# Score products of two attention stages on 128 partitions instead of 64

## The chip, the cores and the metric

The kernel runs on one core of a Trainium2 chip. The metric is the device time of one execution, in microseconds (us), as the median of several runs. TensorE is the matrix engine (PE in the profile, PEld for its weight loads), VectorE is DVE, ScalarE is ACT, GpSimd is POOL, and SyncE (SP) issues most DMAs.

## What is computed

Three blocks on 256 latent tokens (and, in the first layer, 256 context tokens) of 1024 features, all in float32: two layers of a modulated network, then one layer with a hybrid mixer. Two parts matter here.

The first is the differential attention of layer 0. It has 8 heads, each with two maps of 64 features:

```
q, k, v = split(t @ w_in)                    # q, k: 8 heads x 2 maps x 64; v: 8 heads x 128
q, k    = rope(q), rope(k)                   # latent tokens only
sc      = einsum('blhid,bkhid->bihlk', q, k_all) * 64**-0.5
p       = softmax(sc);  p = p[:, 0] - lam * p[:, 1]
o       = rmsnorm(p @ v_all) * (1 - lambda_init)
```

The second is the mixer of the last layer, with 12 heads of 64 features in three groups of 4 (a causal window of 128, strides 4 and 16; four outputs that each join one head of every group) and 8 heads of block attention, which at 256 tokens is plain causal attention:

```
qa, ka, va, qb, kb, vb, g_a, g_b = split(h @ w_in)   # qa, ka, va: 12 x 64; qb, kb, vb: 8 x 64
scores = q @ k.T * 64**-0.5 - slope * distance, masked; softmax; @ v
merged = sigmoid(g_a) * (y_a @ w_up_a) + sigmoid(g_b) * (y_b @ w_up_b)
x      = x + merged @ w_out
```

## The kernel before

Every float32 operand of a product is kept as an exact sum hi + lo of two float32r parts. `split` and `split_scaled` (lines 115 to 122) make them: ACT copies the source to hi, DVE subtracts hi from the source for lo. `mm3` (lines 124 to 128) then forms a product as three matmuls that add up in one PSUM bank: hi hi, hi lo and lo hi. The profile puts these three at L126, L127 and L128, whoever calls them, so they are told apart by tile names and shapes. The shape `64*128 64x256` is a product that contracts over 64 partitions, has 128 weight columns and streams 256 columns.

SBUF tiles of 4 KB per partition come from one arena of 34 buffers (`unit`), PSUM tiles (`ps`) are 8 banks. The program is written in phases. A planner at compile time lays out each engine's queue, close to the order of the source; it puts an instruction that would have to wait behind the next one that need not.

**Differential attention** (`DiffAttention`, from line 861). A head's q and k come from TensorE with features on partitions: 128 partitions are the two maps of 64. `rope_in` and `rope_out` call `parts` once for the 256 context columns (from PSUM) and once for the 256 rotated latent columns (from SBUF), which lays out the operands of the scores. q of map 0 is `[hi0; lo0]` (hi on partitions 0 to 63, lo on 64 to 127), of map 1 `[lo1; hi1]`; k is `[lo0; hi0]`, `[hi1; lo1]`, and `r.hi = [hi0; hi1]`. So one product over 128 partitions (L1015) gives q_hi k_lo + q_lo k_hi, and a second over the 64 partitions of the map (L1016) gives q_hi k_hi:

```
nc.tensor.matmul(sc[:, 0:w], q[:, sb, tq], kk[:, sb, tk], start=True, stop=False)      # L1015
nc.tensor.matmul(sc[:, 0:w], q[pr, sb, tq], khi[pr, tk], start=False, stop=True)       # L1016
```

`scores` runs for 32 items: 8 heads, 2 streams (512 keys for latent queries, 256 for context), 2 tiles of 128 queries. Each item has two maps, and so four products. In every step of the pipeline come `scores` of an item, then `between` (a piece of the projections of later heads, or another filler), `turn` of the item before (transposed probabilities), `values`, and the norm of the output. POOL does a multiplication of the rotation (L943) and the power of the norm (L359).

**Hybrid mixer** (`HybridMixer`, from line 1300). `project` makes 128 columns of x @ w (two heads) with features on partitions, 24 matmuls of 256 columns. `qk` (in `body`) splits them into hi and lo tiles of 128 partitions, one ACT and one DVE instruction a block. 8 such blocks run ahead of the attention, 12 as the fillers of its steps 0 to 11 (`todo`, `each`). `scores` (L1360 to 1374) calls `mm3` on the 64 partitions of one head, `pr = slice(base, base + 64)`. There are 24 items: 16 with one head (the 8 block heads, two query tiles each, 128 or 256 keys), then 8 with three heads that share a softmax, and so nine products on 64 partitions one behind the other. POOL zeroes the ten tiles of v (L1419) at the start of `body`; `place` writes into the first four of them.

Of the kernel before, what the change touches and what calls it, by code (L numbers as in the profile page):

```python
# [13 lines left out]
P = 128  # L14
# [14 lines left out]
class Split:  # L29
    """A float32 operand as an exact sum hi + lo of two float32r parts.  # L30

    Both parts lie in 4 KB/partition units, `kpu` blocks of `width` columns each.
    """
# [25 lines left out]
class Order:  # L59
    """Pieces of independent chains, issued in the order of the times they are due at."""  # L60
# [16 lines left out]
class Kern:  # L77
# [41 lines left out]
    def split_scaled(self, hi, lo, src, scale):  # L119
        """scale: an immediate or a [P,1] column"""  # L120
        self.nc.scalar.activation(hi, src, AF.Copy, scale=scale)
        self.nc.vector.scalar_tensor_tensor(lo, src, scale, hi.bitcast(F32), ALU.mult, ALU.subtract)
# [13 lines left out]
    def wsplit(self, raw, arena=False):  # L136
        """(hi, lo) units"""
# [12 lines left out]
    def wdma256(self, w, c0):  # L150
        """256 columns of a [1024, n] matrix as two halves of the rows: 2 x [P, 4, 256]"""
# [5 lines left out]
    def wcols(self, w, c0, nk=KB):  # L157
        """128 columns of a [128 nk, n] matrix: [P, nk, 128]"""
        return self.wload(w[:, c0:c0 + P].rearrange("(k p) c -> p k c", p=P), [P, nk, P])

    def wrows(self, w, k, arena=False):
        """128 rows of a [n, 1024] matrix: [P, 1024]"""
        return self.wload(w[k * P:(k + 1) * P, :], [P, D], arena)

    def wpair(self, w, kp, c0, n=512, arena=False):
        """256 rows, up to 512 columns: [P, 2, n]"""
# [5 lines left out]
    def setup(self):  # L172
# [6 lines left out]
        # conditioning vectors, as columns: [P, 8, 32], column 0 latent, 1 context  # L179
# [15 lines left out]
        # adds up the two accumulations of each of 2 x 2 rows: [128, shift/scale, stream]  # L195
        self.sel = cp.tile([P, 2, 2], F32, name="sel")
        # sums over the partitions into row 0 or 1
# [15 lines left out]
    def cols(self, src, n, name, rows=None):  # L213
        """n rows of 128 -> [P, n] columns"""
# [11 lines left out]
    def ada_group(self, i, gi, vector=False):  # L226
        """modulation columns 2048*gi ... of layer i, for both streams, as columns; vector: the
        products with each partition's conditioning values on the vector engine"""
# [53 lines left out]
        # whatever this group completes  # L282
# [7 lines left out]
    def fill(self, n=1):  # L290
        """advance the pending adaLN products by n steps"""
# [6 lines left out]
    def mod_a(self, i, j):  # L298
        """(1 + scale) * g_pre of sublayer j (0 ffn, 1 mixer, 2 ffn)"""
# [7 lines left out]
    def mod_g(self, i, j):  # L307
        """weight * gate * g_post of sublayer j"""
# [8 lines left out]
    def gate_rows(self):  # L317
        """the gate vectors that are due to DRAM, from where they can be spread over the partitions"""
# [10 lines left out]
    def spread(self, row):  # L329
        """a vector of 1024 in DRAM on every partition"""  # L330
# [22 lines left out]
    def rstd_of(self, ss, n, width):  # L353
        """(ss / n + eps) ** -0.5 on [P, width]"""
# [7 lines left out]
    def gated(self, h, y, g, half):  # L362
        """h += rmsnorm(y) * g, y as two PSUM halves, the first complete `half` us before the second"""
# [30 lines left out]
    def begin(self, lT, nk, nt, w, tail):  # L394
        """y = lT.T @ w per token tile, whose last `tail` blocks wait for contract()"""
# [22 lines left out]
    def contract(self, c, residual, nxt):  # L418
        """the rest of c; residual(t, y) takes each tile, and nxt starts under the last blocks"""
# [1242 lines left out]
```

## Time and profile before

| | |
|---|---|
| time, median of 3 runs | 2371.59 us (2371.04 to 2375.98) |
| the profiled execution, its span | 2375.7 us |
| TensorE busy | 2331.7 us, 98% |
| VectorE, ScalarE, GpSimd busy | 1373.8, 996.8, 71.7 us |
| differential attention, `scores` | about 480 to 670 us |
| hybrid mixer, first block of `qk` to the last `scores` | about 1975 to 2118 us |

Start times are from the beginning of the span. A matmul's busy time runs from the first column to the modelled end of its last, and successive ones overlap; what a product costs a stage is the distance from its start to the start of the next.

### The profile page before, as it was taken

Reading aid. Unit: us, or ns where it says so; the run is one execution under the profiler, and the core shown is the slowest. Engines: PE = TensorE matmul, PEld = TensorE weight load, DVE = VectorE, ACT = ScalarE, POOL = GpSimd, SP = SyncE. Lnnn points to the kernel's source line nnn. Section 1 sums busy time; section 2 is a strip of 40 time slices with the busy share of each in tenths; the row PEclk is TensorE's granted clock in tenths of the full one; section 3 lists DMA queues with packets and bytes.
Section 4 is the critical chain, followed back from the end, with each engine's and each line's share of the span. In section 5 each row is a group of like instructions: output and inputs, shape, how many; then the busy total and the mean of one; then the engine's idle time right before and its main releaser. Section 6 shows DMA issues by size and latency. Waiting matters only on the chain.

```text
span 2375.7 us, 33808 instructions
## 1 busy us (share of the span) xinstructions
PE 2331.7 (98%) x13435; PEld 1993.5 (84%) x13435; DVE 1373.8 (58%) x2234; ACT 996.8 (42%) x1775; POOL 71.7 (3%) x104
## 2 busy tenths in 40 slices
PE   7999999999999999999999999999999999999998
PEld 5888788887678788888887887689989989998997
DVE  3866324577757663236766326675565556677554
ACT  4322223456544232224222225665445545555443
POOL 0000000001100000000000000100000001000000
PEclk9999999999999999999999999999999999999999
DMA  9655333312663652342655342445665675436654
GB/s 278 204 173 178 119 101 121 99 57 69 210 206 126 184 166 92 106 140 69 198 179 160 107 142 63 139 148 174 194 196 164 187 244 152 138 109 199 176 179 142
DMA packets 270951, 361.46 MB, mean 152 GB/s; under 512 B 11473, under 2 KB 222281, under 8 KB 270793
## 3 DMA queue, kind: packets, MB, share of 16 engines
q1 hardware_dynamic: 270464, 359.17, 48.8%
q8 instruction: 105, 1.72, 0.3%
q14 instruction: 54, 0.43, 0.1%
q10 hardware_dynamic: 328, 0.14, 0.0%
HBM read 355.02 MB, written 4.24 MB: 151 GB/s over the span
## 4 chain that ended last, share of the span: by engine, by line
PE 61%; DVE 4%; DMA 2%; ACT 1%; issue 1%; POOL 1%; POOLq 0%; DVEq 0%; ACTq 0%
PE ps L126 20%; PE ps L127 20%; PE ps L128 20%; DMA raw<-in_ffn_gate_dram 1%; DVE u L117 1%; DMA raw<-in_ada_w_dram 1%; ACT junk L344 1%; DVE u L382 1%; POOL sm L350 1%; DVE s_l L527 0%; PE ps L516 0%; DVE u L504 0%; DVE wl L117 0%; DVE u L245 0%; DVE scr L372 0%
## 5 line engine op out<-in xcount | busy, mean ns | idle before, releaser
L117 DVE TENSOR_TENSOR wl<-raw,wh 128x1024 fp32r<-128x1024 f32 x458 | 550.5, 1210 | 529.9 <-ACT wh L116 528.4
L126 PE MATMUL ps<-s_h,wh 128*128 128x256 f32 (+1 forms) x2560 | 840.0, 329 | 2.8 <-DVE s_h L805 1.9
L127 PE MATMUL ps<-s_l,wh 128*128 128x256 f32 (+1 forms) x2560 | 832.6, 325 | 0.6 <-DVE s_l L527 0.2
L128 PE MATMUL ps<-s_h,wl 128*128 128x256 f32 (+1 forms) x2560 | 831.6, 325 | 0.0
L116 ACT ACTIVATE wh<-raw 128x1024 fp32r<-128x1024 f32 x458 | 474.5, 1047 | 576.3 <-PE ps L127 501.8
L126 PEld LDWEIGHTS ps<-s_h,wh 128*128 128x128 f32 x2560 | 487.4, 191 | 52.9 <-issue 5.4
L127 PEld LDWEIGHTS ps<-s_l,wh 128*128 128x128 f32 x2560 | 487.6, 190 | 41.5 <-DVE s_l L527 2.3
L128 PEld LDWEIGHTS ps<-s_h,wl 128*128 128x128 f32 x2560 | 487.3, 190 | 39.8 <-issue 0.2
L126 PE MATMUL ps<-wh,s_h 128*128 128x512 f32 (+1 forms) x976 | 366.5, 376 | 0.5 <-DVE s_h L526 0.4
L127 PE MATMUL ps<-wl,s_h 128*128 128x512 f32 (+1 forms) x976 | 363.0, 372 | 0.0
L128 PE MATMUL ps<-wh,s_l 128*128 128x512 f32 (+1 forms) x976 | 363.0, 372 | 0.0
L245 DVE SCALAR_TENSOR_TENSOR u<-raw,sc,u 128x1024 f32<-128x1024 f32 x154 | 192.1, 1280 | 90.3 <-DMA raw<-in_ada_w_dram 89.8
L126 PEld LDWEIGHTS ps<-wh,s_h 128*128 128x128 f32 x976 | 183.8, 188 | 35.5 <-ACT u L1018 0.8
L116 ACT ACTIVATE s_h<-scr 128x256 fp32r<-128x256 f32 (+1 forms) x144 | 74.0, 514 | 328.1 <-DVE scr L684 306.2
L128 PEld LDWEIGHTS ps<-wh,s_l 128*128 128x128 f32 x976 | 183.8, 188 | 32.2
L127 PEld LDWEIGHTS ps<-wl,s_h 128*128 128x128 f32 x976 | 183.9, 188 | 31.1
L127 PE MATMUL ps<-u,s_h 128*128 128x512 f32 (+1 forms) x312 | 116.7, 374 | 1.3 <-DVE u L117 1.3
L126 PE MATMUL ps<-u,s_h 128*128 128x512 f32 (+1 forms) x312 | 117.2, 376 | 0.0
L128 PE MATMUL ps<-u,s_l 128*128 128x512 f32 (+1 forms) x312 | 116.5, 373 | 0.0
L684 DVE TENSOR_TENSOR scr<-scr,ps 128x512 f32<-128x512 f32 (+1 forms) x120 | 67.6, 563 | 65.1 <-PE ps L128 65.1
L682 ACT ACTIVATE scr<-ps 128x512 f32<-128x512 f32 (+1 forms) x120 | 58.6, 492 | 107.5 <-PE ps L128 100.8
L117 DVE TENSOR_TENSOR s_l<-scr,s_h 128x256 fp32r<-128x256 f32 (+1 forms) x144 | 78.3, 544 | 33.8 <-ACT s_h L116 33.4
(176 smaller groups left out, 1892.2 us busy)
## 6 DMA issues: line engine op xcount, KB each, us to landing
raw<-in_ffn_w_in_dram SPq DMA_DIRECT2D x176, 512.0 KB, 4.8
raw<-in_ada_w_dram SPq DMA_DIRECT2D x144, 512.0 KB, 4.4
raw<-in_ffn_w_out_dram SPq DMA_DIRECT2D x88, 512.0 KB, 3.5
raw<-in_ffn_gate_dram SPq DMA_DIRECT2D x44, 512.0 KB, 4.9
raw<-in_ffn_up_dram SPq DMA_DIRECT2D x44, 512.0 KB, 4.8
raw<-in_ffn_down_dram SPq DMA_DIRECT2D x44, 512.0 KB, 4.5
raw<-in_w_in_dram SPq DMA_DIRECT2D x44, 512.0 KB, 3.8
raw<-in_da_w_in_dram SPq DMA_DIRECT2D x24, 512.0 KB, 4.0
```

Source lines behind the costliest of these rows:

```text
L116: self.nc.scalar.activation(hi, src, AF.Copy)
L117: self.nc.vector.tensor_tensor(lo, src, hi.bitcast(F32), ALU.subtract)
L126: mm(out, lhi, rhi, start=start, stop=False)
L127: mm(out, lhi, rlo, start=False, stop=False)
L128: mm(out, llo, rhi, start=False, stop=stop)
L245: nc.vector.scalar_tensor_tensor(acc[s][h], raw, x, acc[s][h], ALU.mult, ALU.add)
L344: self.nc.scalar.activation(self.junk, src, AF.Square, scale=1.0 / 32, accum_out=ss)
L350: nc.gpsimd.tensor_tensor(r, v, self.mhalf, ALU.pow)
L382: nc.vector.scalar_tensor_tensor(h[:, sl], st.yg[k], st.r, h[:, sl], ALU.mult, ALU.add)
L682: self.nc.scalar.activation(sg, pg[:, 0:T], AF.Silu)
L684: self.nc.vector.tensor_tensor(hf, sg, pu[:, 0:T], ALU.mult)
```

## The change

In the differential attention, `r.hi` becomes two tiles of 128 partitions with zeros on the half that isn't the map's: `[hi0; 0]` and `[0; hi1]`. The second product of a map then contracts over 128 partitions with all of `q[:, sb, tq]`, and the zeros cancel the lo half. POOL writes the zeros (two `memset` of 64 x 512 for each head); ACT makes hi in two instructions of 64 partitions instead of one of 128. In the mixer, every head gets tiles of its own on 128 partitions, in the same way: q as `[hi; lo]` (or `[lo; hi]`), k once as `[lo; hi]` and once as hi on the head's own half with zeros on the other. The first product of the two gives hi lo + lo hi, the second hi hi: two products on 128 partitions in place of three on 64. For that `qk` now runs two ACT and two DVE instructions for a block of q, four ACT and two DVE for a block of k, each on 64 partitions. The tiles of q and k take 15 arena buffers instead of 12, and POOL gets ten `memset` ahead of those of v. The rest of the diff takes out comments.

```diff
@@ rope_in
         if r.part:
-            r.hi = k.unit([P, 512], F32R)
+            r.hi = k.unit([P, 2, 512], F32R)
+            for m in range(2):
+                nc.gpsimd.memset(r.hi[64 - 64 * m:128 - 64 * m, m, :].bitcast(F32), 0.0)
@@ parts
-        if r.part:
-            nc.scalar.activation(r.hi[:, c], src, AF.Copy)
         for m in range(2):
             p, o = half[m], half[1 - m]
             if r.part:
+                nc.scalar.activation(r.hi[p, m, c], src[p, :], AF.Copy)
                 nc.scalar.activation(r.dst[o, m, c], src[p, :], AF.Copy)
-                nc.vector.tensor_tensor(r.dst[p, m, c], src[p, :], r.hi[p, c].bitcast(F32), ALU.subtract)
+                nc.vector.tensor_tensor(r.dst[p, m, c], src[p, :], r.hi[p, m, c].bitcast(F32), ALU.subtract)
@@ DiffAttention scores
-                pr = slice(64 * sb, 64 * sb + 64)
-                nc.tensor.matmul(sc[:, 0:w], q[pr, sb, tq], khi[pr, tk], start=False, stop=True)
+                nc.tensor.matmul(sc[:, 0:w], q[:, sb, tq], khi[:, sb, tk], start=False, stop=True)
@@ HybridMixer scores
-                k.mm3(sc[:, 0:wd], qT.at(0, pb, t * P, (t + 1) * P)[pr, :], qT.at(1, pb, t * P, (t + 1) * P)[pr, :],
-                      kT.at(0, pb, 0, wd)[pr, :], kT.at(1, pb, 0, wd)[pr, :], True, True)
+                u, b = n // 4, n % 4
+                qn = q[u][:, b, t * P:(t + 1) * P]
+                nc.tensor.matmul(sc[:, 0:wd], qn, kk[0][u][:, b, 0:wd], start=True, stop=False)
+                nc.tensor.matmul(sc[:, 0:wd], qn, kk[1][u][:, b, 0:wd], start=False, stop=True)
@@ HybridMixer body
-        qa, ka = k.asplit(6, S), k.asplit(6, S)
-        qb, kb = k.asplit(4, S), k.asplit(4, S)
+        heads4 = lambda n: [k.unit([P, 4, S], F32R) for _ in range(n)]
+        qa, ka = heads4(3), [heads4(3) for _ in range(2)]
+        qb, kb = heads4(2), [heads4(2) for _ in range(2)]
+        for x in ka[1] + kb[1]:
+            for m in range(2):
+                nc.gpsimd.memset(x[64 - 64 * m:128 - 64 * m, m::2, :].bitcast(F32), 0.0)
...
-        def qk(dst, x, c0, scale):
-            p = self.project(c0 + x * P)
-            k.split_scaled(dst.at(0, x), dst.at(1, x), p, scale)
+        def qk(dst, x, c0, is_q):
+            src = self.project(c0 + x * P)
+            for m in range(2):
+                n = 2 * x + m
+                u, b = n // 4, n % 4
+                p, o = slice(64 * m, 64 * m + 64), slice(64 - 64 * m, 128 - 64 * m)
+                if is_q:
+                    k.split_scaled(dst[u][p, b, :], dst[u][o, b, :], src[p, :], 0.125)
+                else:
+                    k.split(dst[1][u][p, b, :], dst[0][u][p, b, :], src[p, :])
+                    nc.scalar.activation(dst[0][u][o, b, :], src[p, :], AF.Copy)
```

## Rows read from the trace of the kernel before

**Rows 1.** The page, part 1: busy time of each engine, share of the span, instructions.
```profile
PE 2331.7 (98%) x13435; PEld 1993.5 (84%) x13435; DVE 1373.8 (58%) x2234; ACT 996.8 (42%) x1775; POOL 71.7 (3%) x104
```

**Rows 2.** Busy time by stretch; after the engines granted clock, DMA share, GB/s.
```profile
480.00:670.00 190.00, 189.50 (x1198) 141.99 (x1197) 139.56 (x392) 109.97 (x286) 19.99 (x26) 1.00 0.38 121
1975.00:2125.00 150.00, 150.00 (x1156) 142.59 (x1155) 104.05 (x238) 76.78 (x180) 0.00 (x0) 1.00 0.49 140
...
540.00:560.00 20.00, 20.00 (x133) 16.98 (x134) 16.93 (x51) 13.21 (x39) 2.85 (x4) 1.00 0.10 27
2020.00:2040.00 20.00, 20.00 (x158) 18.97 (x157) 14.07 (x35) 10.71 (x27) 0.00 (x0) 1.00 0.38 106
```

**Rows 3.** Groups by line and shape on TensorE: count, busy us, mean ns.
```profile
L1016 PE MATMUL ps<-u,u 64*128 64x512 f32 x32 | 15.9, 495 | 0.0
```

**Rows 4.** Timeline of TensorE, an item of 512 keys: start us, duration, line.
```profile
522.50 0.40 PE L1015 MATMUL ps<-u,u 128*128 128x512 f32 x1
522.83 0.49 PE L1016 MATMUL ps<-u,u 64*128 64x512 f32 x1
...
524.11 0.39 PE L126 MATMUL ps<-s_h,wh 128*128 128x256 f32 x1
524.33 0.28 PE L127 MATMUL ps<-s_l,wh 128*128 128x256 f32 x1
```

**Rows 5.** The same view, an item of 256 keys.
```profile
557.68 0.28 PE L1015 MATMUL ps<-u,u 128*128 128x256 f32 x1
...
559.05 0.28 PE L127 MATMUL ps<-s_l,wh 128*128 128x256 f32 x1
```

**Rows 6.** The same view, two products of 512 columns on 128 partitions.
```profile
2053.10 0.39 PE L127 MATMUL ps<-wl,s_h 128*128 128x512 f32 x1
2053.32 0.39 PE L128 MATMUL ps<-wh,s_l 128*128 128x512 f32 x1
```

**Rows 7.** The same view, mixer, one head and 128 keys, with its neighbours.
```profile
2021.57 0.27 PE L128 MATMUL ps<-u,u 128*128 128x128 f32 x1
2021.78 0.32 PE L126 MATMUL ps<-s_h,s_h 64*128 64x128 f32 x1
...
2022.26 0.38 PE L126 MATMUL ps<-s_h,wh 128*128 128x256 f32 x1
2022.48 0.28 PE L127 MATMUL ps<-s_l,wh 128*128 128x256 f32 x1
2022.60 0.28 PE L128 MATMUL ps<-s_h,wl 128*128 128x256 f32 x1
```

**Rows 8.** The same view, mixer, one head and 256 keys, first and last.
```profile
2025.55 0.38 PE L126 MATMUL ps<-s_h,s_h 64*128 64x256 f32 x1
...
2026.32 0.28 PE L127 MATMUL ps<-s_l,wh 128*128 128x256 f32 x1
```

**Rows 9.** The same view, mixer, three heads and 256 keys: nine products.
```profile
2077.75 0.38 PE L126 MATMUL ps<-s_h,s_h 64*128 64x256 f32 x1
...
2079.24 0.28 PE L127 MATMUL ps<-s_l,wh 128*128 128x256 f32 x1
```

**Rows 10.** Timelines of ACT and DVE, a weight split of a q or k block.
```profile
1983.89 1.06 ACT L116 ACTIVATE wh<-raw 128x1024 fp32r<-128x1024 f32 x1 [1.38 <-issue]
...
1984.99 1.22 DVE L117 TENSOR_TENSOR wl<-raw,wh 128x1024 fp32r<-128x1024 f32 x1 [1.12 <-ACT wh L116]
```

**Rows 11.** Timelines of ACT and DVE, one half of a k in `parts`.
```profile
528.00 0.38 ACT L931 ACTIVATE u<-ps 64x256 fp32r<-64x256 f32 x1
...
528.41 0.42 DVE L932 TENSOR_TENSOR u<-ps,u 64x256 fp32r<-64x256 f32 x1
```

**Rows 12.** L504 and L1419: shortest, median, longest in ns; then the longest L504.
```profile
L504 DVE TENSOR_SCALAR u<-u,sm x56: 477/485/2031, 8.8 to 2182.8; 128x512 f32<-128x512 f32 x56
...
L1419 POOL MEMSET u<- x10: 949/954/1227, 1964.5 to 1973.1; 128x1024 f32 x10
...
1964.56 2.03 DVE L504 TENSOR_SCALAR u<-u,sm 128x512 f32<-128x512 f32 x1 [0.73 <-POOL sm L350]
```

More of the change, by code (lines that the diff above doesn't have):

```diff
@@ L1361, in scores @@
             it.e = e = k.unit([P, len(grp), S])
-            for g, (qT, kT, pb, base, pat, slope, v) in enumerate(grp):
-                pr = slice(base, base + 64)
+            for g, (q, kk, n, pat, slope, v) in enumerate(grp):
                 sc = k.ps()
-                k.mm3(sc[:, 0:wd], qT.at(0, pb, t * P, (t + 1) * P)[pr, :], qT.at(1, pb, t * P, (t + 1) * P)[pr, :],
-                      kT.at(0, pb, 0, wd)[pr, :], kT.at(1, pb, 0, wd)[pr, :], True, True)
+                u, b = n // 4, n % 4
+                qn = q[u][:, b, t * P:(t + 1) * P]
+                nc.tensor.matmul(sc[:, 0:wd], qn, kk[0][u][:, b, 0:wd], start=True, stop=False)
+                nc.tensor.matmul(sc[:, 0:wd], qn, kk[1][u][:, b, 0:wd], start=False, stop=True)
                 nc.vector.scalar_tensor_tensor(e[:, g, 0:wd], self.pats[pat // 2][:, pat % 2, t, 0:wd], slope,
@@ L1395, in values @@
             ng = len(hd.grp)
-            for g, (qT, kT, pb, base, pat, slope, v) in enumerate(hd.grp):
+            for g, (q, kk, n, pat, slope, v) in enumerate(hd.grp):
                 p = hd.pT[g]
@@ L1439, in vt @@
             return [[z[n // 4][:, (n % 4) * 2 + b, :] for b in range(2)] for z in dst]
-        def qk(dst, x, c0, scale):
-            p = self.project(c0 + x * P)
-            k.split_scaled(dst.at(0, x), dst.at(1, x), p, scale)
+        def qk(dst, x, c0, is_q):
[9 more added lines that the diff above has]
+                    nc.scalar.activation(dst[0][u][o, b, :], src[p, :], AF.Copy)
         for x in range(4):
-            qk(qb, x, 2304, 0.125)
-            qk(kb, x, 2816, 1.0)
+            qk(qb, x, 2304, True)
+            qk(kb, x, 2816, False)
             if x == 0:
@@ L1452, in body @@
         for x in range(6):
-            todo.append(lambda x=x: qk(qa, x, 0, 0.125))
-            todo.append(lambda x=x: qk(ka, x, 768, 1.0))
+            todo.append(lambda x=x: qk(qa, x, 0, True))
+            todo.append(lambda x=x: qk(ka, x, 768, False))
         todo.append(lambda: values(1536, 512, va, 0))
@@ L1458, in body @@
         jobs = [
-            (yb, x, [[(qb, kb, x, 64 * q, 3, 2.0 ** -(2 * x + q + 1), vt(vb, 2 * x + q))] for q in range(2)])
+            (yb, x, [[(qb, kb, 2 * x + q, 3, 2.0 ** -(2 * x + q + 1), vt(vb, 2 * x + q))] for q in range(2)])
             for x in range(4)]
@@ L1492, in body @@
                     n = 4 * g + 2 * x + q
-                    grp.append((qa, ka, n // 2, 64 * (n % 2), g, 2.0 ** (-8.0 * (n + 1) / 12), vt(va, n)))
+                    grp.append((qa, ka, n, g, 2.0 ** (-8.0 * (n + 1) / 12), vt(va, n)))
                 heads.append(grp)
```

## The prediction, made before the change was run

> **What bounds the kernel now.** I read the page first: TensorE is busy 98% of the span, the next engine, VectorE, 58% [rows 1]. That is an average over stages, so the second view is busy time by stretch, for the two stages that the change touches: differential attention from 480 to 670 us, the mixer's q and k blocks and scores from 1975 to 2125. TensorE is idle for 0.5 and 0.0 us there, at a granted clock of 1.00 (2.4 GHz), while VectorE is busy 139.6 of 190 and 104.1 of 150 us, ScalarE less [rows 2]. So both stages go at the pace of TensorE's starts, and a product that costs less there shortens the kernel, as long as VectorE keeps up. Third, the groups by shape give the products on 64 partitions, one row for them all [rows 3]. Their mean duration (495 ns) says little, because durations overlap. Fourth, the timeline of TensorE gives what counts, the distance from start to start.
>
> On 128 partitions a product of 256 columns starts 0.12 us after the one before (the last two of [rows 7]), one of 512 columns 0.22 [rows 6]. In an item of 512 keys, L1015 and L1016 alternate, and the distances are 0.33 and then 0.43 us each (1.28 for three), and even the projection that follows needs 0.22 in place of 0.12 [rows 4]. In the mixer, distances inside a run of products on 64 partitions are normal: nine of them and the one after take 1.49 us [rows 9], ten at 0.12 would be 1.2. The extra comes at both ends: 0.21 into the run, 0.21 to 0.22 out of it [rows 7]. So the pause belongs to the change between 64 and 128 contracted partitions, not to the 64 partitions as such. In the differential attention there is such a change at every product.
>
> **The sum on TensorE, differential attention.** 32 items (8 heads, 2 streams, 2 query tiles), four products each, as many after the change as before. With 512 keys, from the first start to the second start after the item: 524.33 - 522.50 = 1.83 us [rows 4]. Without pauses 4 x 0.22 + 0.12 = 1.00. Saved 0.83, 16 times: 13.3 us. With 256 keys 559.05 - 557.68 = 1.37 us [rows 5], without pauses 5 x 0.12 = 0.60, saved 0.77, 16 times: 12.3. Together 25.6 us.
>
> **The sum on TensorE, mixer.** Two products replace three. One head, 128 keys, from the start of the product before to the second start after: 2022.48 - 2021.57 = 0.91 us [rows 7]; after the change four distances of 0.12, 0.48; saved 0.43, 8 items: 3.4. One head, 256 keys, from its first start: 0.77 us [rows 8], after 3 x 0.12 = 0.36, saved 0.41, 8 items: 3.3. Three heads: 1.49 us [rows 9], after 7 x 0.12 = 0.84, saved 0.65; the four items of 256 keys and the four of 128 taken alike: 5.2. Together 11.9 us, of which 40 x 0.12 = 4.8 are the 40 products that go and the rest pauses. Both stages: 37.5 us.
>
> **What is added beside TensorE.** Half a tile costs ACT and DVE what a whole one does, since the columns are the same: 0.38 and 0.42 us for 64 x 256 [rows 11]. Differential attention: one more ACT instruction in each of the 16 calls of `parts` for a k, 6.1 us on an engine that is busy 110 of 190 [rows 2]; DVE gets nothing. Mixer: a q block gets one more on ACT and one on DVE, a k block three and one; 10 blocks each, so 40 x 0.38 = 15.2 us of ACT and 20 x 0.42 = 8.4 us of DVE, in about the first half of the stretch: 8 blocks of 24 x 0.12 us, then 12 steps of some 4 us (2025.55 - 2021.57, [rows 7, 8]) with a block each. All of it lies beside TensorE's products, so I cost it at nothing while DVE has room. Does it? In 2020 to 2040 DVE is busy 14.07 [rows 2]; five steps with a block each add 2.1, while the stretch shrinks by about 2.1 to 17.9: 90%. In 540 to 560 it is 16.93 already, and three items' savings leave 17.6: 96%. Over the whole stage 139.6 of 164.4 is 85%. So DVE stays under 100% everywhere, but with little room in a few stretches. Give-back between 0 and 11 us (second rival); I take 2.5, near the lower end, because the stage as a whole has 25 us of DVE time left and fillers on TensorE can be moved by about a step.
>
> L932 begins when L931 ends [rows 11], though it doesn't read what L931 writes; I take it that two engines' reads of one PSUM bank are kept apart. Then a k block's six instructions go in order, with four hand-overs between the engines; behind each waits whatever stands next in that queue, mostly the next block's weight split of 1.06 and 1.22 us [rows 10]. ACT has 1.38 us of slack per block and DVE 1.12 in front of these splits [rows 10], and a block's PSUM bank is one of eight. I cost that at 0 unless the queues lock (last rival).
>
> **POOL.** It gets 16 memsets of 64 x 512 in the differential attention and 10 in the mixer. No row has that size; 128 x 1024 takes 954 ns [rows 12], so between nothing and 954 ns, and half, 0.48, as my estimate by the columns. In the differential attention POOL is busy 20 of 190 us [rows 2]; behind a memset on its queue wait the rotation's multiplication and the norm's power, each needed a step later, and the scores wait for the memset itself, which is issued with the evacuation of k, a step or more ahead of them. Cost 0. In the mixer the ten stand before the ten of L1419, which run without a break from 1964.5 [rows 12]. So `place` gets its zeros up to 4.8 us later. It holds two PSUM banks, and behind it on ACT and DVE stand the last blocks of the normalized input, for which TensorE would wait. Between 0 and 4.8; I take 0.5, since the planner puts an instruction that waits behind those that need not. The longest L504, 2031 ns against a median of 485, begins at 1964.56, beside the first memset [rows 12], which bounds what a memset does to a DVE instruction beside it: 1.5 us, from which comes the third rival. The three more arena buffers: by my count of live tiles the mixer needs at most 34 of 34 (30 before) in its steps 5 to 7; no wait follows, but if one does, a block's evacuation slips by up to a step; 0 to 3 us, taken as 0.
>
> **The result of the sum.** 37.5 - 2.5 - 0.5 = 34.5 us. The profiled execution's span is 2375.7 us, 0.17% above the median of the runs, 2371.59, so no scaling is needed. 2371.6 - 34.5 = 2337.
>
> **Rivals.** *VectorE sets the pace in places.* If DVE can't be busier than in the fullest stretch, 16.93 of 20 [rows 2], 540 to 560 gives nothing, and added up over the ten stretches of 20 us in this stage about 8 of the 25.6 us are lost; in 2020 to 2040, 16.2 us of DVE need 19.1, so 1.2 of 2.1 are lost, some 3 in the 48 us of the 12 steps. 26.5 us remain: 2345. For it: DVE's share of 85% there. Against: the stage's mean.
>
> *The memsets take DVE's time.* If each of the 26 holds a DVE instruction for its 0.48 us and DVE is the bound there, 12.5 us are given back: 2371.6 - 37.5 + 12.5 = 2347. For it: the 2031 ns. Against: L504 is a long scalar operation from SBUF to SBUF, of which the stage with 16 of the memsets has only tiny ones. The Trainium skill speaks here against the change (SBUF — State Buffer, Who interferes with whom): GpSimd shares a port pair with VectorE, and an instruction that takes it blocks the other engine for its whole length; but by the same section operations with a source in PSUM or two sources don't clash with a pure write. By the first half the time would be 2347, by the second the sum above stays; the one row agrees with the first half, and no run here shows the second yet.
>
> *The pause is not due to the number of partitions* but to what the pair does (one bank, twice the same weights' address, or a stride). Then only the 40 products go: 2371.6 - 4.8 plus small losses, 2367 to 2371. Against it: nine products into shared banks without a pause inside [rows 9], and the ordinary projections add up in one bank as well.
>
> *Evacuation locks the queues* (slower). If every hand-over of a block in the mixer waits behind a weight split of the other engine (mean 1.14), a k block needs 4 x 0.38 + 2 x 0.42 + 4 x 1.14 = 6.9 us, a q block with three hand-overs 5.0, against 24 x 0.12 = 2.88 on TensorE. The excess is 10 x 4.0 + 10 x 2.1 = 61 us: 2395. It decides from 4.8 us a block on average, where it eats all 37.5. Against: the slack of more than 1.1 us in front of each split [rows 10], and weights are split ahead.
>
> **Chances.** Forecast 0.62, VectorE 0.22, memsets 0.06, pause not removed 0.05, queues locked 0.05. The first three are faster, so faster 0.90, same 0.05, slower 0.05; the bound between them is 0.2%, about what a measurement of this kernel can tell from no change. The range reaches down to 2330 (nothing given back, 2334, and a planned order that happens to fall well) and up to 2350, which holds the second and third case.
>
> **What would show it.** In the profile after: L1015 to L1016 at 0.22 and 0.12 us with no extra distance into the next projection; two products a head in the mixer at 0.12; about 40 products fewer; DVE over 85% in the differential attention, with TensorE still without idle time. TensorE waiting for ACT or DVE there would be the second rival, distances still at 0.3 to 0.4 us the fourth, TensorE idle between 1975 and 2046 the last. The prediction would be wrong above all if the planned order of the queues, which I can't see in advance, came out differently for the whole stage.

## The result and the profile of the changed kernel

The changed kernel takes 2346.83 us in the median of 4 runs (2345.72 to 2348.98), the kernel before 2373.62 in the same comparison (2371.04 to 2375.98): 0.989 of it, 95% interval 0.988 to 0.990. That is 1.1% faster, inside the forecast range of 2330 to 2350, 10 us above the forecast value of 2337, and nearer to the second and third rivals' 2345 and 2347.

The profiled execution has a span of 2344.6 us, 31.1 less than that of before. The engines' busy time, share and instructions on its page, and then the busy time by stretch (the lines that answer to [rows 1] and [rows 2]):

```profile
PE 2297.3 (98%) x13395; PEld 1981.4 (85%) x13395; DVE 1381.5 (59%) x2254; ACT 1017.9 (43%) x1831; POOL 84.3 (4%) x130
```

```profile
480.00:670.00 190.00, 185.01 (x1283) 151.29 (x1282) 144.71 (x417) 120.97 (x313) 27.47 (x40) 1.00 0.44 144
1975.00:2125.00 150.00, 147.56 (x1188) 144.38 (x1188) 118.83 (x273) 92.35 (x217) 0.00 (x0) 1.00 0.52 152
540.00:560.00 20.00, 18.71 (x146) 17.66 (x145) 15.61 (x50) 13.54 (x40) 2.76 (x4) 1.00 0.01 1
```

TensorE has 40 instructions fewer, as forecast. But it is now idle for 5.0 of 190 and 2.4 of 150 us in the two stages, where it had been idle for 0.5 and 0.0. VectorE isn't full either: 76% in the attention, and 15.61 of 20 us in the stretch for which the prediction expected 96%.

Where the time went is read from the powers of the norm (L350 on GpSimd), one group of which stands at each end of a phase. The differential attention lasts from the first line to the second, the mixer from the third to the fourth. Before:

```profile
404.88 0.55 POOL L350 TENSOR_TENSOR sm<-sm,mhalf 128x1 f32<-128x1 f32 x1 [4.61 <-DVE sm L349]
697.92 0.56 POOL L350 TENSOR_TENSOR sm<-sm,mhalf 128x1 f32<-128x1 f32 x1 [14.22 <-DVE sm L349]
1963.97 0.55 POOL L350 TENSOR_TENSOR sm<-sm,mhalf 128x1 f32<-128x1 f32 x1 [8.54 <-DVE sm L349]
2174.05 1.46 POOL L350 TENSOR_TENSOR sm<-sm,mhalf 128x1 f32<-128x1 f32 x1 [200.01 <-DVE sm L349]
```

After:

```profile
401.74 0.55 POOL L350 TENSOR_TENSOR sm<-sm,mhalf 128x1 f32<-128x1 f32 x1 [4.61 <-DVE sm L349]
680.34 0.56 POOL L350 TENSOR_TENSOR sm<-sm,mhalf 128x1 f32<-128x1 f32 x1 [14.72 <-DVE sm L349]
1943.19 0.55 POOL L350 TENSOR_TENSOR sm<-sm,mhalf 128x1 f32<-128x1 f32 x1 [8.50 <-DVE sm L349]
2143.75 0.55 POOL L350 TENSOR_TENSOR sm<-sm,mhalf 128x1 f32<-128x1 f32 x1 [185.01 <-DVE sm L349]
```

The attention went from 293.0 to 278.6 us (14.4 saved, forecast 25.6 less 2.5), the mixer from 210.1 to 200.6 (9.5 saved, forecast 11.9 less 0.5). The other 7.1 us of the 31.1 lie in phases that didn't change. About half of that is TensorE's clock: in the kernel before, the granted clock was 0.50 in two stretches of 3.4 us outside the two stages, each behind a wait of TensorE (1.98 us until 241.65, 2.75 until 1295.75), and products of 512 columns started 0.43 us apart there in place of 0.23, so each stretch cost 1.7 us. The changed kernel has none there.

```profile
242.00:245.30 3.30, 3.30 (x11) 2.62 (x9) 0.79 (x7) 0.00 (x0) 0.00 (x0) 0.50 0.78 263
```

Phases that didn't change differ by some microseconds from one execution to the next (the first power above stands at 401.6 to 408.4 us in the profiles of this study), so below it is the two stages that are compared, beside the medians.

**The pauses are gone.** TensorE's timeline in the changed kernel: an item of 512 keys and one of 256, each from its first score product to the second start after it, as [rows 4] and [rows 5] were read (the scores are now L1016 and L1017):

```profile
607.40 0.40 PE L1016 MATMUL ps<-u,u 128*128 128x512 f32 x1
...
608.44 0.28 PE L127 MATMUL ps<-s_l,wh 128*128 128x256 f32 x1
...
594.64 0.28 PE L1016 MATMUL ps<-u,u 128*128 128x256 f32 x1
...
595.23 0.28 PE L127 MATMUL ps<-s_l,wh 128*128 128x256 f32 x1
```

1.04 us in place of 1.83 and 0.59 in place of 1.37; the forecast was 1.00 and 0.60. In the mixer, three heads with 256 keys take 0.92 us, where [rows 9] had 1.49 and the forecast 0.84:

```profile
2060.65 0.36 PE L1367 MATMUL ps<-u,u 128*128 128x256 f32 x1
...
2061.57 0.28 PE L127 MATMUL ps<-s_l,wh 128*128 128x256 f32 x1
```

**New waits came.** What TensorE's queue waited for between 470 and 670 us (line, releaser, us in total, times, longest), and then between 1975 and 2125:

```profile
PE ps L942 <- DVE u L934: 1.4, 3, 0.5
PE ps L1016 <- ACT u L1019: 1.3, 2, 0.8
PE ps L455 <- DVE scr L1027: 0.9, 2, 0.6
PE ps L942 <- DVE u L937: 0.7, 2, 0.4
...
PE ps L1386 <- DVE u L1376: 2.1, 3, 1.3
PE ps L127 <- DVE u L117: 0.3, 1, 0.3
```

Before, the first window held one such wait, 0.5 us on a DMA. Now the rotation's product (L942) waits for the end of `parts` (L934, L937), the scores for the exponential that frees a bank (L1019), the transposes for the combined probabilities (L1027), and the mixer's transposes (L1386) for VectorE's scaling (L1376). Idle time shows only part of such a wait: a product of 256 columns is held busy for 0.28 us but followed after 0.12, so the first 0.16 us of a late start are covered. Therefore I added up distances from start to start, from the first score to the transposes of the next phase, by what follows what (my sums over TensorE's timeline, us):

```
                                            before   after   difference
score -> score                               32.2     18.1     -14.1
score -> product of 256 columns               9.6      5.0      -4.5
score -> anything else                        3.4      3.2      -0.2
product of 256 -> product of 256             84.8     81.7      -3.1
anything else -> score                        9.3     12.9      +3.5
anything -> rotation                          3.5      5.6      +2.1
anything -> transposes, sums of squares      25.3     26.9      +1.6
the rest                                     59.3     59.1      -0.2
sum                                         227.4    212.4     -15.0
```

The first four lines are the pauses: 21.9 us. The next three are late starts: 7.2 us given back. A part of both is the planned order, which cuts the score products into 40 runs in place of 36: four distances fewer inside the runs, and four entries more.

### The profile page after: what moved, and what is told of

The parts are those of the page before. It is cut to its first block, busy times and chain, and to the rows that moved or that the text cites. A ratio compares the mean times of both kernels' runs of the same rounds, so it can differ in the third digit from the quotient of the medians.

```text
span 2344.6 us, 33841 instructions
## 1 busy us (share of the span) xinstructions
PE 2297.3 (98%) x13395; PEld 1981.4 (85%) x13395; DVE 1381.5 (59%) x2254; ACT 1017.9 (43%) x1831; POOL 84.3 (4%) x130
## 4 chain that ended last, share of the span: by engine, by line
PE 60%; DVE 5%; ACT 2%; issue 1%; DMA 1%; POOL 1%; POOLq 0%; DVEq 0%; ACTq 0%
PE ps L126 19%; PE ps L127 19%; PE ps L128 19%; DVE u L117 1%; DVE wl L117 1%; DMA raw<-in_ffn_gate_dram 1%; ACT junk L344 1%; DVE u L382 1%; ACT wh L116 0%; DVE s_l L527 0%; POOL sm L350 0%; PE ps L516 0%; ACT u L116 0%; DVE scr L372 0%; PE ps L262 0%
## 5 line engine op out<-in xcount | busy, mean ns | idle before, releaser
L350 POOL TENSOR_TENSOR sm<-sm,mhalf 128x1 f32<-128x1 f32 x50 | 27.5, 553 | 1996.2 <-DVE sm L349 1996.2
```

Source lines behind the costliest of these rows:

```text
L350: nc.gpsimd.tensor_tensor(r, v, self.mhalf, ALU.pow)
```

## The experiments

The theories, as the expectations number them: 1, the evacuation of a k, one ACT instruction longer in each call of `parts`, comes late; 2, VectorE's work as a whole doesn't fit under a TensorE that needs less time; 3, the memsets on GpSimd hold VectorE up; 4, the planned order, which leaves a dependent product a given number of products behind what it needs; v1's expectation adds one on the number of the evacuation's instructions. All times in one table; ratio and interval are against the kernel before on the same chip, "attention" and "mixer" are the stages as above, each read from one profile. Where the same code of a stage stands in several kernels, the attention differs by 0.5 us (278.1, 278.5, 278.6) and the mixer by 1.1 (199.5 to 200.6).

| kernel | median us (range) | ratio, interval | attention | mixer |
|---|---|---|---|---|
| before | 2373.62 (2371.04 to 2375.98) | | 293.0 | 210.1 |
| changed | 2346.83 (2345.72 to 2348.98) | 0.989 (0.988 to 0.990) | 278.6 | 200.6 |
| e1_diff_only | 2365.07 (2364.52 to 2366.38) | 0.995 (0.994 to 0.997) | 278.1 | 218.2 |
| e2_mixer_only | 2365.11 (2360.93 to 2365.79) | 0.995 (0.994 to 0.997) | 292.8 | 200.4 |
| e3_old_parts | 2347.99 (2345.05 to 2350.66) | 0.988 (0.986 to 0.990) | 276.6 | 200.1 |
| e4_no_memset | 2349.24 (2348.50 to 2350.04) | 0.988 (0.986 to 0.990) | 277.8 | 200.2 |
| e5_short_max | 2343.32 (2340.00 to 2346.60) | 0.988 (0.986 to 0.989) | 272.0 | 200.4 |
| e6_before_short_max | 2368.16 (2365.75 to 2369.42) | 0.998 (0.997 to 0.999) | 288.9 | 209.9 |
| v1_sbuf_parts | 2358.48 (2358.05 to 2364.28) | 0.995 (0.993 to 0.996) | 287.2 | 200.3 |
| g1_step_later | 2351.21 (2348.53 to 2352.95) | 0.991 (0.989 to 0.992) | 280.7 | 200.1 |
| g2_step_later_short_max | 2345.40 (2344.08 to 2348.01) | 0.988 (0.987 to 0.990) | 276.7 | 200.4 |
| v2_pool_split | 2357.15 (2355.44 to 2360.65) | 0.993 (0.991 to 0.995) | 288.7 | 199.5 |
| v3_pool_split_both | 2358.29 (2355.19 to 2359.25) | 0.993 (0.990 to 0.995) | 288.9 | 196.8 |
| v4_mixer_pool | 2344.41 (2343.73 to 2345.23) | 0.987 (0.986 to 0.989) | 278.5 | 197.2 |

Six of these kernels have stretches within the two stages in which the granted clock was 0.50 (1.2 GHz) in place of 1.00 (2.4 GHz), and each goes with a wait of TensorE, in all but one within 1.2 us behind it: one in the attention of g1 (behind a wait of 2.06 us), one in g2 (1.32), three in v1 (2.64, 3.67 and 1.66), two each in v2 and v3 (all 2.43 to 2.45) and one in the mixer of e1, which began during a wait of 7.62. Other waits, of 1.81 and 1.74 us in v2, had no such stretch behind them. The one in g1, TensorE's timeline and then the busy time with the granted clock behind the engines:

```profile
613.05 0.47 PE L1016 MATMUL ps<-u,u 128*128 128x512 f32 x1 [2.06 <-ACT u L932]
613.60 0.62 PE L1016 MATMUL ps<-u,u 128*128 128x512 f32 x1
614.02 0.63 PE L1017 MATMUL ps<-u,u 128*128 128x512 f32 x1
```

```profile
613.80:617.10 3.30, 3.30 (x15) 3.11 (x15) 2.24 (x8) 2.08 (x6) 0.00 (x0) 0.50 0.41 166
```

Products of 512 columns start 0.42 us apart there, not 0.23. Each stretch lasts 3.4 us (7 in e1) and, at half the pace, costs TensorE about 1.7 us by my estimate: 1.7 us in g1 and g2, 5.1 in v1, 3.4 in v2 and v3, and 2.3 in e1 (4.6 us from the end of the wait). The two stages of the other kernels in the table have no such stretch.

### Each half of the change alone: e1_diff_only, e2_mixer_only

The class `HybridMixer` of the kernel before in the changed kernel, and `DiffAttention` of the kernel before in it.

> The change in the differential attention alone, the mixer as before. Between the profiles of before and after, the differential attention got 14.4 us shorter (697.92 - 480.2 less 680.34 - 477.0 on the power of the next norm) and the mixer 9.5. If the two parts don't act on each other, this kernel stands 13 to 16 us under the kernel before, about 2359, and the mixer's stage takes what it took before, 210 us. If the mixer's gain hangs on an earlier entry, less.

> The change in the mixer alone, the differential attention as before. Additive parts: 9 to 11 us under the kernel before, about 2363, the differential attention at 229 us from its first score to the next norm.

By stages the halves add up: the attention gains 14.9 us with the old mixer, the mixer 9.6 with the old attention, 14.4 and 9.5 together. But e1 as a whole is 6 us slower than expected, and that is its mixer, whose code is unchanged: 218.2 us in place of 210.1. GpSimd's, VectorE's and TensorE's timelines at the mixer's start in e1, and the first two at the same place in the changed kernel:

```profile
1946.09 8.98 POOL L1420 MEMSET u<- 128x1024 f32 x10
1946.17 9.57 DVE L504 TENSOR_SCALAR u<-u,sm 128x512 f32<-128x512 f32 x2 [0.73 <-POOL sm L350]
...
1955.41 1.97 PE L516 MATMUL ps<-ident,u 128*128 128x128 f32 x8 [7.62 <-DVE u L504]
```

```profile
1943.77 1.57 DVE L504 TENSOR_SCALAR u<-u,sm 128x512 f32<-128x512 f32 x2 [0.73 <-POOL sm L350]
1943.80 5.98 POOL L1423 MEMSET u<- 64x512 f32 x10
```

In e1 the scaling of the norm's rows (L504) began 0.08 us after the first of ten memsets and ended after the last; one instruction of 0.48 us took 9.18, and TensorE stood for 7.6 us; then the granted clock was 0.50 until 1960.0. In the kernel before L504 began 0.09 us behind the first memset too, but took 2.03 us [rows 12], some two memsets; what decides between the two lengths, no run here shows. In the changed kernel L504 began 0.03 us before the memsets, and both instructions took 1.57. So about 1 us of the mixer's gain (TensorE's waits for L504 after 1964, 0.48 and 0.52 us before, none after) comes from the order of these starts, not from the score products. It is the same order in every profile with the changed mixer.

### Evacuation and memsets: e3_old_parts, e4_no_memset

e3 gives `parts` one whole copy of k's hi again, without memsets, and the second product reads it on 128 partitions; e4 makes two whole copies, with no memsets.

In e3, ahead of the loop over the two maps:

```diff
+        if r.part:
+            nc.scalar.activation(r.hi[:, c], src, AF.Copy)
...
-                nc.scalar.activation(r.hi[p, m, c], src[p, :], AF.Copy)
```

In e4, in the loop:

```diff
-                nc.scalar.activation(r.hi[p, m, c], src[p, :], AF.Copy)
+                nc.scalar.activation(r.hi[:, m, c], src, AF.Copy)
```

> All of the change, but r.hi stays one tile of 128 partitions, made by one ACT copy as before, without memsets; the second product of a map takes all 128 partitions of it (so it adds lo of one map times hi of the other, and the scores are not the reference's). TensorE does the same work as after the change, ACT 16 copies and POOL 16 memsets less. Theory 1, the longer evacuation of k (one more ACT instruction and hand-over in each call of parts, and the memsets) holds TensorE up: 6 to 11 us shorter than after the change, 2336 to 2341, and the rotation's product no longer waits for DVE. Theory 2, VectorE and the score chain have no room for a faster TensorE whatever parts does: within 3 us of after the change, 2344 to 2350.

> All of the change but for the 16 memsets of the differential attention: ACT copies all 128 partitions into both tiles of r.hi, at the same cost by the columns (so the half that should be zero holds the other map, and the scores are not the reference's). Theory 3, the memsets hold up the power of the norm and the rotation on POOL: VectorE's wait for the power falls from 6.8 us to 3, and the time by 3 to 6 us. Theories 1 and 2: no change beyond 2 us from after the change, about 2346.

The attention takes 276.6 and 277.8 us. One ACT instruction a call and the memsets together are worth 2.0 us, the memsets alone no more than 0.8, little more than the spread. Theories 1 and 3 don't carry the 11 us that are missing. In e3 the waits moved rather than went: the rotation's product still waits 1.4 us, the transposes of the output's norm for ACT 0.8. Theory 3's own sign didn't come either: VectorE's waits for the power of the norm make 8.7 us in e4 (14 waits) and 9.1 in the changed kernel (14), against 3.6 (6) in the kernel before.

### VectorE's time: e5_short_max, e6_before_short_max

```diff
-                nc.vector.tensor_reduce(nm[:, sb:sb + 1], sc[:, 0:w], AX.X, ALU.max, negate=True)
+                nc.vector.tensor_reduce(nm[:, sb:sb + 1], sc[:, 0:64], AX.X, ALU.max, negate=True)
```

> All of the change, and in the differential attention VectorE takes the maximum over the first 64 keys instead of 256 or 512 (the softmax is the same in exact numbers, since any shift cancels). That takes some 22 us off VectorE (0.69 and 0.42 us to about 0.2, 32 each) and shortens the wait from scores to exponential, and nothing off TensorE. Theory 2, VectorE's time holds back TensorE: the stage from the norm before to the norm after, 278.6 us after the change, falls by 7 to 10 us, the time to some 2338. Theory 4, what is missing lies in TensorE's own steps or the planned order: within 2 us of after the change.

> The kernel before with the same short maximum: the control. Where TensorE alone sets the pace, 22 us less on VectorE buy nothing: within 2 us of the kernel before, the stage at 293 us. The gain of the change in this stage is then what lies between this run and the one with the change and the short maximum: 22 to 25 us by theory 2, about 14 by theory 4.

Between 480 and 670 us VectorE is busy 131.5 us in e5 (144.7 in the changed kernel) and 124.3 in e6 (139.6). The attention takes 272.0 and 288.9: the change saves 16.9 us with the short maximum and 14.4 without it. All that TensorE's queue still waits for in e5 in that stretch:

```profile
PE ps L942 <- DVE u L937: 1.5, 3, 0.6
PE ps L942 <- DVE u L934: 0.9, 2, 0.5
```

The scores and transposes are on time again, the rotation isn't. So VectorE's maximum explains some 2.5 us of what the change gives back, no more; it is a part of VectorE's load and a link of the chain from scores to exponential, and these runs don't separate the two. The kernel before was not free of late starts either: there the short maximum saved 4.1 us, though its TensorE had been idle for 0.5.

### Fewer, longer instructions: v1_sbuf_parts

One ACT copy of all 512 columns to SBUF, the rotation there, and `parts` once over 512 columns in place of twice over 256.

> All of the change, with another evacuation in the differential attention: one ACT copy of all 512 columns of q or k to SBUF, the rotation of the latent half there, then parts once over 512 columns instead of twice over 256. The rotation's product no longer shares its bank with pending reads of parts, DVE does 64 instead of 128 instructions there at 0.69 instead of 2 x 0.42 us (5 us less in all), ACT about as much as after the change. Theory 5, the bank shared by the rotation's product and parts is what stops TensorE: the stage falls by 3 to 5 us, the time to some 2342. Theory 2: by 1 to 3 us, from DVE's 5 us less.

The attention takes 287.2 us, 8.6 more than the changed kernel. TensorE's waits there:

```profile
PE ps L1016 <- DVE u L117: 6.7, 3, 3.7
PE ps L1016 <- ACT u L1019: 2.8, 3, 1.7
```

It is the scores that wait, for a bank that a split of transposed probabilities or an exponential frees, and behind three of these waits the granted clock was 0.50, which makes some 5.1 of the 8.6 us. Work saved in total is no gain when it stands in one block in front of what the scores need.

### The planned order: g1_step_later, g2_step_later_short_max

```diff
-                    late.append(lambda: self.rope_out(r))
+                    late.append((k.step, lambda: self.rope_out(r)))
...
-            if late:
-                late.pop(0)()
+            k.step = step
+            if late and late[0][0] + 2 <= step:
+                late.pop(0)[1]()
```

> The change, with the rotation of a q or k block asked for one step later (two steps behind the block's second half instead of one); nothing else differs, and it computes the same. In the order of TensorE's queue the columns of products between a block's last product and its rotation then make 4.6 to 8.8 us, mean 6.2, for the twelve blocks in the heads' steps, against 3.1 to 6.4, mean 5.0, in the changed kernel. Theory of the order (the queue's order leaves a dependent product a fixed number of products behind what it needs; without the pauses these products pass in less time, and the evacuation chain is as long as ever): the rotation's waits (2.1 us idle, 3.05 us in the distances of starts) all but go, the stage takes 275 to 276 in place of 278.6, and the run is 2 to 3.5 us shorter than the changed kernel, 2343 to 2345. Theory of VectorE's time (the sum of its work in a step is what doesn't fit): the lateness only moves to the scores and the transposes, the stage stays at 278 to 279 and the run at 2346 to 2348. Slower than that only if the block's PSUM bank, held a step longer, makes the scores wait.

> As the run before, and the maximum of a map is taken over its first 64 keys alone (part of the computation left out: the bias of the exponential is not the row's maximum), which takes some 20 us off VectorE in this stage. The changed kernel with the short maximum alone has a stage of 272.0, with 4.0 us of extra distance at ten rotations. Theory of the order: these 4 us go as well, the stage takes 268 to 269.5, and nothing but a few tenths remains between it and the forecast by the pauses (before 293.0 less 25.6 = 267.4). Theory of VectorE's time: with VectorE this light the rotation's lateness should not be there at all, so moving it changes nothing: 271.5 to 272.5.

The rotation's waits went as theory 4 says, from 2.1 us to 0.4, but the stage got 2.1 us longer in g1 and 4.7 in g2 (against e5), some 1.7 of it in each by a granted clock of 0.50. TensorE's waits in g1:

```profile
PE ps L1016 <- ACT u L1019: 2.3, 3, 1.2
PE ps L1016 <- ACT u L932: 2.1, 1, 2.1
...
PE ps L942 <- DVE u L937: 0.4, 1, 0.4
```

The scores now wait for `parts` and for banks. As far as theory 4 promised a gain from more distance (275 to 276 us in g1, 268 to 269.5 in g2) it falls, also without the clock: less 1.7 us, by my estimate, the stages take 279.0 and 275.0, and one wait of 1.7 us on a DMA in g2 doesn't make up the rest. The distance is taken from another chain.

### VectorE's time without a shorter chain: v2_pool_split, v3_pool_split_both, v4_mixer_pool

```diff
-        self.split(hi, lo, raw)
+        if pool:
+            self.nc.scalar.activation(hi, raw, AF.Copy)
+            self.nc.gpsimd.tensor_tensor(lo, raw, hi.bitcast(F32), ALU.subtract)
+        else:
+            self.split(hi, lo, raw)
```

v2 does this for heads 2 to 7 of the attention, v4 for the twelve q and k blocks that run as fillers of the mixer's steps 0 to 11, v3 for both.

> The change, with the lo parts of the weights of heads 2 to 7 (12 subtractions of 128x1024, 1.22 us each on VectorE) taken by GpSimd, which is busy 27 of 190 us in this stage; it computes the same. VectorE loses 14.6 us, about as much as the short maximum took off it (144.7 to 131.5 of 190), but no chain of a head gets shorter: weights are split ahead. GpSimd gets 12 instructions of, by the 0.81 us of its 128x256 multiplication, some 3.2 us each, and the norm's power and the rotation's multiplication wait behind one now and then. Theory of VectorE's time (its sum in a step is what makes TensorE's starts late): as with the short maximum, the stage takes 272 to 274 and the run 2340 to 2343. Theory of the length of the chains (reduction, exponential, combination, or a block's evacuation, one after another, against a step of TensorE that became 0.8 us shorter): nothing is gained, the stage takes 277 to 280, 2345 to 2349, a little worse where a power or a multiplication waits behind a split.

> As the run before, and the 12 weight splits of the mixer's first q and k blocks (about 1.15 us each on VectorE) go to GpSimd too, behind the 20 memsets. Theory of VectorE's time: the 2.1 us for which the mixer's transposes wait for VectorE's scaling go, the mixer takes 198 to 199 in place of 200.6. Theory of the chains' length: 200 to 201. If the splits on GpSimd are too late for the products that read them, TensorE waits for the lo part of a weight and the mixer gets longer, by up to 12 times some 1 us.

> The change, with the weight splits' lo parts of the mixer's first twelve q and k blocks on GpSimd, as in the run before, and the differential attention as in the changed kernel; it computes the same. The run before had the mixer at 196.8 us (from the second to the third power of the norms around it) against 200.6 in the changed kernel, with TensorE no longer waiting for the scaling of the probabilities, while its differential attention was 10 us longer. If the stages are independent: mixer 197, differential attention 278 to 279, the run 2342 to 2344. If the mixer's gain came from what the stage before left behind (weights loaded and split earlier, as the kernel was late): mixer 200, the run 2346 to 2348.

In the attention it made the stage 10 us longer, and not by GpSimd's queue (VectorE's waits for the power fell from 9.1 us to 4.3). The timelines of GpSimd and VectorE in v2 (L146 is the moved subtraction, L1061 a multiplication of two columns in the output's norm, L1057 in the changed kernel):

```profile
514.51 2.38 POOL L146 TENSOR_TENSOR wl<-raw,wh 128x1024 fp32r<-128x1024 f32 x1 [6.85 <-ACT wh L145]
514.55 2.35 DVE L1061 TENSOR_TENSOR sm<-sm,sm 128x2 f32<-128x2 f32 x1
```

The shortest, median and longest in ns of L1061 and of the rotation's multiplication and sum on VectorE:

```profile
L1061 DVE TENSOR_TENSOR sm<-sm,sm x16: 142/161/2360, 501.7 to 675.5; 128x2 f32<-128x2 f32 x16
L948 DVE TENSOR_TENSOR scr<-ps,u x16: 410/418/426, 440.4 to 638.5; 128x256 f32<-128x256 f32 x16
L950 DVE TENSOR_TENSOR scr<-scr,scr x16: 410/416/2473, 442.2 to 639.0; 128x256 f32<-128x256 f32 x16
```

TensorE's waits for `parts` before the rotation's product, which is L946 here:

```profile
PE ps L946 <- DVE u L941: 8.1, 6, 2.4
PE ps L946 <- DVE u L938: 4.9, 3, 1.8
```

A multiplication of 0.16 us that starts beside a subtraction on GpSimd lasts until the other ends. The Trainium skill has this (SBUF — State Buffer, Who interferes with whom): a VectorE instruction with both inputs in SBUF shares a read port with a GpSimd instruction that reads SBUF, one with an input in PSUM doesn't, and a pure write doesn't disturb it. This trace agrees: L1061 and L950 (both inputs in SBUF) reach 2.4 us, L948 (one in PSUM) never exceeds 0.43, and a multiplication of the same shape and inputs (L1060) that runs beside a memset of the changed kernel, three times, stays at 0.16. So VectorE was not relieved (146.4 us busy in the window), and v2 can't tell theory 2 from the others. It does show how short the chains' slack is: the rotation waits 13 us in all, and behind two of these waits the granted clock was 0.50, some 3.4 of the 10 us.

In the mixer the same move is a gain: 196.8 us in v3 and, with the attention of the changed kernel, 197.2 in v4, 3.3 less than in the changed kernel. TensorE's waits between 1975 and 2125 us in v4 are one line:

```profile
PE ps L127 <- DVE u L117: 0.3, 1, 0.3
```

In the busy time of the same stretch VectorE has 112.75 us in place of 118.83:

```profile
1975.00:2125.00 150.00, 149.75 (x1207) 147.00 (x1206) 112.75 (x267) 94.57 (x222) 25.38 (x11) 1.00 0.52 155
```

The wait for the scaling is gone, so VectorE's time was what the mixer's gain lacked. v4, which leaves nothing out, takes 2344.41 us, 0.987 of the kernel before, 2.4 less than the changed kernel. The two were not run side by side, and the intervals of their ratios overlap; each stands against the kernel before, 29.0 and 26.8 us below it. The 3.3 us of the stage are beyond the spread.

## Why the prediction was right, and where it was off

**The mechanism: right.** The pause belongs to the change between 64 and 128 contracted partitions. In e3 the second product reads other data over 128 partitions, with the evacuation of before, and the gain is there as well; the item's distances are the forecast ones to 0.04 us. The rival with a pause of another origin falls.

**The attention's 25.6 us: 3.7 too much.** The term that was mis-sized is "16 times" for each kind of item: two items that are followed by a projection ([rows 4], [rows 5]) stood for all. Of 36 runs of score products in the kernel before, 26 are followed by a product of 256 columns; this exit fell from 0.37 to 0.18 us on average, and the distance behind it from 0.22 to 0.12. The other 10 are followed by a product with 32 weight columns (8) or a transpose (2), where the exit fell only from 0.34 to 0.26 us: 3.4 us for 10 before, 3.2 for 12 after. The normal distance of two score products of 512 columns is 0.23, not the 0.22 of [rows 6], and the four runs more pay their own exits. Behind a product of one column an item takes 0.1 us more, but before (1.93 us with 512 keys) and after (1.14) alike, so the saving is the same there.

**The give-back: 2.5 forecast for both stages, 7.2 measured in the attention alone**, inside the bounds of 0 to 11. That the total landed in the range is owed to its width, which took in the second and third rivals. The second rival's size (about 8 in the attention) was closer, its mechanism was not: in 540 to 560, where the prediction expected VectorE at 96%, it is busy 15.61 of 20 us, less than before, and TensorE is idle all the same. What the prediction treated as a sum of work (85% of the stage, so there is room) is a matter of chains in queues that run in order. One place shows it, in the changed kernel (timelines of ACT, DVE and PE; L932 copies, L934 subtracts in `parts`):

```profile
522.76 0.38 ACT L932 ACTIVATE u<-ps 64x256 fp32r<-64x256 f32 x1 [0.44 <-DVE u L934]
524.51 0.16 DVE L1060 TENSOR_TENSOR sm<-sm,sm 128x2 f32<-128x2 f32 x1 [0.90 <-POOL sm L359]
524.71 0.43 DVE L934 TENSOR_TENSOR u<-ps,u 64x256 fp32r<-64x256 f32 x1
525.19 0.70 PE L942 MATMUL ps<-scr,u 128*128 128x256 f32 x2 [0.55 <-DVE u L934]
```

The copy that L934 needs ended by 523.14, but L934 stands behind L1060, which waits 0.90 us for a power on GpSimd; VectorE stands still, and TensorE after it. Shown by runs: 2.5 us of the give-back go with VectorE's maximum (e5, e6), 2.0 with the longer evacuation and its memsets (e3), and neither can simply be had by moving the rotation (g1, g2). These two shares may overlap, and what is left, some 3 us, is late starts of several chains, none above 1.4 us of idle time in total. VectorE's waits for this power grew from 3.6 to 9.1 us with the change, and not by the memsets (8.7 in e4). But that such a wait is the common cause of the late starts was read at this place and not tried, and stays open.

**The mixer's 11.9 us: right in size, cut by VectorE.** With twelve weight splits off VectorE the stage takes 12.8 us less than before, of which about 1 is the earlier start of L504: 11.8 remain. Their nearness to 11.9 is in part luck, since v4 also takes work off VectorE that the kernel before had. In the changed kernel the prediction's "nothing while DVE has room" failed at three transposes that waited 2.1 us for L1376. The 90% forecast for 2020 to 2040 was not the critical stretch: the longest of these waits, 1.3 us, ends at 1987, in the first steps.

**The memsets: right for the attention** (0.8 us at most, forecast 0). In the mixer the forecast was that `place` gets its zeros late, at 0 to 4.8 us. ACT did wait for them, 2.1 us at 1950.70, and TensorE did not. What was missed is who starts first beside L504: ahead of the memsets in the changed mixer, a gain of 1 us. And the prediction's bound for what a memset does to an instruction beside it, 1.5 us, does not hold: in e1 L504 lost 8.7 us and TensorE 7.6. The third rival's 2347 is the nearest number of all, but its cause is not the one: without the 16 memsets of the attention (e4) at most 0.8 us come back.

**The queues did not lock**: between 1975 and 2046 TensorE waits for the transposes' scaling, as told, and otherwise for 0.3 us. The sum of the steps: 8.7 us less in the attention than forecast (25.6 - 2.5 - 14.4), 1.9 less in the mixer (11.9 - 0.5 - 9.5), 2.8 more in phases that didn't change (26.8 by the medians less 14.4 and 9.5, rounded), and the kernel before at 2373.6 in place of 2371.6: 8.7 + 1.9 - 2.8 + 2.0 = 9.8, the distance from 2337 to 2346.8.

## What to carry to other kernels

Where products that contract over 64 and over 128 partitions alternate, read the distances from start to start on both sides of each change; making them all 128 with zeros is worth about 0.2 us a change here (an item with four of them went from 1.83 to 1.04 us), even where columns and instructions stay the same, but count it for each kind of neighbour. When the bound engine gets faster in a planned pipeline, share of busy time is a poor guide to the give-back: list the products that wait for a chain through two in-order queues, and expect a few tenths of a microsecond from each. Where a change makes TensorE wait longer at one place, read the granted clock behind that wait too, before the whole loss is put down to the wait itself. And when work goes to GpSimd, look at what VectorE does at that moment and where its inputs lie.

## What the runs showed of the hardware

- One VectorE instruction with its input in SBUF (L504, 0.48 us alone) that began 0.08 us into ten memsets on GpSimd that ran back to back was held through all of them in e1, 9.18 us; in the kernel before, 0.09 us into such a run, it took 2.03; started 0.03 us ahead of them, two took 1.57. The Trainium skill (SBUF — State Buffer, Who interferes with whom) says that whoever issues first has the shared port pair for the whole instruction; e1 shows that it can stay with GpSimd over a run of instructions.
- In v2 a multiplication of 128x2 on VectorE took 2.36 us in place of 0.16 beside a subtraction of 128x1024 on GpSimd, which itself took 2.4 us where VectorE needs 1.22.
- A pause in TensorE's starts remains where score products of 128 partitions stand beside products of one column, transposes or 32 weight columns: the first distance behind a product of one column is 0.31 to 0.33 us for 512 columns (542.01 to 542.34 in the changed kernel) and 0.20 for 256, in place of 0.23 and 0.12.
- Behind waits of TensorE of 1.32 to 3.67 us in g1, g2, v1, v2 and v3 the granted clock was 0.50 for 3.4 us, with starts 0.42 and 0.21 us apart for 512 and 256 columns in place of 0.23 and 0.12; behind others, up to 1.81 us in v2, it stayed at 1.00.
